# Last feed-forward layer: gate and up of 18 blocks as a 2x2 block product with seven multiplications

## The chip, the cores and the metric

One core of a Trainium2 chip runs the whole program in one launch. The metric is device time in microseconds (us). The kernel before took 1428.83 us, the median of three runs (1427.67 to 1429.59). The engines are TensorE (PE, with its weight loads PEld), VectorE (DVE), ScalarE (ACT), GpSimd (POOL) and SyncE (SP, which issues the weight loads); each works through its own queue in order.

## The reference

Two residual layers over a sequence of 512 rows of width 1024: an even layer (Mamba-2 scan and differential attention), an odd layer (S5 scan and latent attention), and behind each a SwiGLU feed-forward block; a final RMSNorm ends it. What the change touches is the second feed-forward block:

```
def rms_norm(x, g):
    y = xf * lax.rsqrt(jnp.mean(xf * xf, axis=-1, keepdims=True) + NORM_EPS)
    return (y * g.astype(F32)).astype(x.dtype)
def swiglu(x, wg, wu, wd):
    return (jax.nn.silu(x @ wg) * (x @ wu)) @ wd
h = h + swiglu(rms_norm(h, norm_ffn[i]), ffn_gate[i], ffn_up[i], ffn_down[i])
```

The hidden width is 2816, which is 22 blocks of 128. All arrays are float32.

## The kernel before

**Tiles.** The activations lie transposed: `h[i]`, i = 0..7, holds 128 features by 512 rows. A float32 product is made of three TensorE products: each operand is split into a high part in the format float32r and the remainder (`wsplit` for weights, `split_x` for activations: ScalarE casts, VectorE subtracts), and `mm3` adds hi·hi, hi·lo and lo·hi in one PSUM bank (L178, L179, L180). The operands of the feed-forward block are h times the gain, not yet normalised; the factor 1/rms of each row (`rbc`) is multiplied in afterwards.

**Units.** The work is a list of units. A unit is one output tile of 128 features by 512 rows: eight k-steps of three matmuls, 24 matmuls of 512 columns. Gate and up of one hidden block are two units. `ev_g` multiplies the gate by `rbc` on VectorE, applies SiLU on ScalarE, and multiplies by `rbc` on GpSimd (`padd`, L305); `ev_u` multiplies up and gate on VectorE, and `split_x` makes `hid{j}` of it. The 22 blocks go in three parts of 8, 7 and 7 (`PARTS`); behind each part the down projection adds its share to `h`. In the last part the first down unit is 512 columns wide and the others come as 256-column halves, with transposes, the final norm and the stores between them (`last_down`, `last_norm`, `finish`).

**Weights.** `wload` brings the weights of one hidden block, gate and up, as one DMA of 1 MB into one of two `raw` tiles (a row per partition: 1024 columns of gate, then 1024 of up). `wsplit` writes to `whi` and `wlo`, two buffers each; down weights with a `keep` number go to tiles `kh1..7` and `kl1..7` of the pool `fin`, which hold them for both halves.

**Order.** `drive` goes through the list and calls `prep` (load and split) for the next unit before `compute` of this one. This is only the order in which the instructions are written. The order within each engine's queue is made when the program is built: a planner plays the program through with durations of its own and gives each engine the earliest-written instruction that is ready by then, so later-written work can go ahead of earlier work that waits. What comes out of it is fixed; on the chip an engine does not change it.

Of the kernel before, what the change touches and what calls it, by code (L numbers as in the profile page):

```python
# [9 lines left out]
F32 = mybir.dt.float32  # L10
F32R = mybir.dt.float32r
# [7 lines left out]
P = 128  # L19
# [87 lines left out]


PARTS = (8, 7, 7)
CHUNKS = _chunks()  # L110
CH, WLEN = {}, {}
for _k, (_f, _p) in CHUNKS.items():
# [9 lines left out]
class Trunk:  # L122
    def __init__(self, ctx, tc, a, out):
        self.ctx, self.tc, self.nc, self.a, self.out = ctx, tc, tc.nc, a, out
        self.n = 0
# [28 lines left out]
    def wload(self, key):  # L154
        flat, off, n = CH[key]
        raw = self.t(self.wraw, [P, 2048], "raw")
        self.nc.sync.dma_start(out=raw[:, :sum(n)],
                               in_=self.a[flat][off:off + P * sum(n)].rearrange("(p n) -> p n", p=P))
        return raw

    def wsplit(self, raw, o, nk, cw, keep=None):
# [29 lines left out]

    def prep(self, u):
        if "w" in u:
            return
        if u["keep"] in self.kept:
            u["w"] = self.kept[u["keep"]]
            return
        if u["key"] not in self.raws:
            self.raws[u["key"]] = self.wload(u["key"])
        o = sum(CH[u["key"]][2][:u["sub"]])  # L200
        self.left[u["key"]] -= 1
        u["w"] = self.wsplit(self.raws[u["key"]], o, u["nk"], u["m"], u["keep"])
        if u["keep"] is not None:
            self.kept[u["keep"]] = u["w"]
# [48 lines left out]
    def drive(self, items):  # L253
        us = [x for x in items if isinstance(x, dict)]
        nxt = {id(u): v for u, v in zip(us, us[1:])}
        seen = set()
        for u in us:
            if u["keep"] is None or u["keep"] not in seen:
                self.left[u["key"]] = self.left.get(u["key"], 0) + 1
            seen.add(u["keep"])  # L260
        self.order = list(self.left)
        self.prep(us[0])
        for x in items:
            if isinstance(x, dict):
                if id(x) in nxt:
                    self.prep(nxt[id(x)])
                self.fetch()
                self.compute(x)
            else:
                x()  # L270
        self.flush()
# [122 lines left out]
    def setup(self):  # L394
# [9 lines left out]
        nc.gpsimd.memset(self.t(pad, [P, PAD], "pad")[:, 0:1], 0.0)  # L404
        self.pp = {n: self.pool(ctx, "ps_" + n, b, PSUM) for n, b in (("mm", 2), ("sc", 2), ("tp", 2), ("po", 2))}
        self.n_unit = 0
        self.raws, self.kept, self.left = {}, {}, {}
        self.queue, self.held = [], None
        self.cst_sb = self.t(cp, [P, NCST], "cst")
        self.par_sb = self.t(cp, [P, NPAR], "par")  # L410
# [561 lines left out]
        return items  # L972


    def ffn(self, l, E, gain, back=None):
        nc, a = self.nc, self.a
        V, A, G = nc.vector, nc.scalar, nc.gpsimd
# [2 lines left out]
        F = {}  # L980
        st2 = E["st2"] = {"acc": None}
        mt = ("mm", "sc")

        def start():
            F["p"] = self.pool(ctx, f"ff{l}")
            self.norm_done(E)

        def ev_g(j, ps):
# [5 lines left out]
        def ev_u(j, ps):  # L994
            gt = F["gt", j]
            V.tensor_tensor(out=gt, in0=ps, in1=gt, op=ALU.mult)  # L996
            F["hid"].append(self.split_x(F["p"], f"hid{j}", gt, None))
        items, j0 = [], 0
        for pi, nj in enumerate(PARTS):
# [3 lines left out]
            for j in range(nj):  # L1003
                items += [self.unit(f"g{l}_{j0 + j}", n, xs8, (lambda ps, j=j, e=e: e(j, ps)), mt)
                          for n, e in enumerate((ev_g, ev_u))]
                if back is not None:
                    items.append(back)
# [6 lines left out]
            if last and gain == "nfin":  # L1014
                def du(i, hfs):
# [30 lines left out]
    def last_norm(self, i, hf):  # L1046
        nc, st = self.nc, self.fin
        h = self.h[i][:, 256 * hf:256 * hf + 256]
        hg = self.t(self.finp, [P, 256], "hg", bufs=3)
        nc.scalar.activation(out=hg, in_=h, func=AF.Identity, scale=self.par("nfin", i))  # L1050
        sq = self.t(self.finp, [P, 256], f"fsq{hf if i == 0 else 2 + i % 2}")
        if i == KD - 1:
            nc.vector.tensor_tensor(out=sq, in0=h, in1=h, op=ALU.mult)
        else:
# [499 lines left out]
        return items  # L1554


@with_exitstack
def tile_trunk(ctx, tc, a, out):
    k = Trunk(ctx, tc, a, out)
# [18 lines left out]
    def open_fin():  # L1578
        c2.close()
        k.finp = k.pool(c4, "fin")  # L1580
        k.otm = k.t(k.finp, [P, 4, D], "otm")
# [97 lines left out]
```

## Time and profile before

| | us |
|---|---|
| median of the runs | 1428.83 |
| the profiled execution, its own time | 1427.25 |
| its span, from the first to the last instruction | 1425.4 |
| TensorE busy in the span | 1378.2 |
| VectorE busy | 932.9 |
| ScalarE busy | 665.0 |
| GpSimd busy | 225.4 |

The profile is of one execution. Times in the rows are microseconds unless marked ns. A matmul's duration includes its way through the array, so successive matmuls overlap; how fast they follow one another is read from their starts. The waits name what ended an engine's idle time.

### The profile page before, as it was taken

To read this page: it belongs to the slowest core of one execution; us is meant where nothing else is said; L and a number is where in the kernel's file an instruction comes from. 1 tells how busy PE (TensorE), PEld (TensorE's weight loads), DVE (VectorE), ACT (ScalarE), POOL (GpSimd) and SP (SyncE) were. 2 spreads that over 40 slices of the span, in tenths; PEclk is the share of its full clock that TensorE was granted. 3 is DMA by queue.
4 is the path that set the end of the run, shared out by engine and by line. 5 is a ranking of instruction groups with operands and counts; after the bars stand their busy time and mean duration, and the time that the engine had idled before them with its cause. 6 is when DMAs were issued, how large, how long until landed. Compare 5 with 4: busy or idle time off the path is not lost.

```text
span 1425.4 us, 18242 instructions
## 1 busy us (share of the span) xinstructions
PE 1378.2 (97%) x6947; PEld 1136.5 (80%) x6947; DVE 932.9 (65%) x1936; ACT 665.0 (47%) x1177; POOL 225.4 (16%) x184
## 2 busy tenths in 40 slices
PE   8999999999999989999999998989999999999997
PEld 5877878888888868887888786766788888888887
DVE  6987888878766994336766678887663433343454
ACT  7658787967643442233324432278452312222242
POOL 0234500000003101011011214510031101101111
PEclk9999999999999999999999999999999999999999
DMA  5221121121222222232232233220132232232221
GB/s 187 77 78 60 60 89 60 45 74 60 89 89 106 89 83 96 92 115 74 90 109 73 99 113 93 74 78 30 60 118 89 89 112 95 86 107 89 98 95 59
DMA packets 26102, 124.07 MB, mean 87 GB/s; under 512 B 3056, under 2 KB 7792, under 8 KB 14880
## 3 DMA queue, kind: packets, MB, share of 16 engines
q1 hardware_dynamic: 24656, 121.09, 24.7%
q10 hardware_dynamic: 1360, 1.83, 0.4%
q8 instruction: 54, 0.88, 0.3%
q14 instruction: 32, 0.26, 0.1%
HBM read 118.71 MB, written 4.19 MB: 86 GB/s over the span
## 4 chain that ended last, share of the span: by engine, by line
PE 71%; DVE 19%; ACT 5%; issue 2%; POOL 1%; DMA 1%; SPq 0%; ACTq 0%; DVEq 0%; POOLq 0%
PE mm L178 14%; PE mm L179 13%; PE mm L180 13%; PE sc L180 7%; PE sc L179 7%; PE sc L178 7%; DVE wlo L170 3%; DVE qsw L634 2%; ACT whi L169 1%; PE sc L1444 1%; PE po L879 1%; POOL xs L305 1%; ACT qsw L790 1%; PE po L1470 1%; PE mm L774 1%
## 5 line engine op out<-in xcount | busy, mean ns | idle before, releaser
L169 ACT CAST whi<-raw 128x1024 fp32r<-128x1024 f32 (+5 forms) x231 | 224.1, 970 | 530.3 <-PE mm L179 286.2
L170 DVE TENSOR_TENSOR wlo<-raw,whi 128x1024 fp32r<-128x1024 f32 (+5 forms) x231 | 263.3, 1140 | 32.4 <-ACT whi L169 22.6
L305 POOL TENSOR_TENSOR gt<-gt,rbc 128x512 f32<-128x512 f32 x44 | 76.2, 1732 | 573.1 <-ACT gt L991 573.1
L305 POOL TENSOR_TENSOR sacc<-sacc,sq 128x512 f32<-128x512 f32 x29 | 45.4, 1564 | 394.1 <-ACT sq L292 381.6
L996 DVE TENSOR_TENSOR gt<-mm,gt 128x512 f32<-128x512 f32 x44 | 30.4, 690 | 106.6 <-PE mm L180 103.3
L990 DVE TENSOR_TENSOR gt<-sc,rbc 128x512 f32<-128x512 f32 x44 | 30.4, 690 | 83.1 <-PE sc L180 83.0
L1011 DVE TENSOR_TENSOR h<-h,mm 128x512 f32<-128x512 f32 x20 | 13.7, 686 | 54.3 <-PE mm L180 54.3
L178 PE MATMUL mm<-x0h,whi 128*128 128x512 f32 (+2 forms) x91 | 39.1, 429 | 9.5 <-ACT whi L169 6.3
L1011 DVE TENSOR_TENSOR h<-h,sc 128x512 f32<-128x512 f32 x20 | 13.7, 687 | 47.2 <-PE sc L180 47.2
L180 PE MATMUL mm<-x0h,wlo 128*128 128x512 f32 (+2 forms) x91 | 36.8, 404 | 3.6 <-DVE wlo L170 3.6
L991 ACT ACTIVATE gt<-gt 128x512 f32<-128x512 f32 x44 | 27.6, 627 | 23.5 <-DVE gt L990 23.5
L790 ACT ACTIVATE qsw<-mm 32x512 f32<-32x512 f32 x64 | 37.7, 589 | 1.0 <-DVE qraw L786 0.2
L178 PE MATMUL mm<-x7h,whi 128*128 128x512 f32 (+2 forms) x95 | 37.1, 390 | 0.0
L180 PE MATMUL mm<-x7h,wlo 128*128 128x512 f32 (+2 forms) x95 | 37.0, 390 | 0.0
L179 PE MATMUL mm<-x7l,whi 128*128 128x512 f32 (+2 forms) x95 | 37.0, 389 | 0.0
L179 PE MATMUL mm<-x0l,whi 128*128 128x512 f32 (+2 forms) x91 | 36.6, 403 | 0.0
L178 PE MATMUL mm<-x1h,whi 128*128 128x512 f32 (+2 forms) x91 | 36.1, 396 | 0.0
L180 PE MATMUL mm<-x1h,wlo 128*128 128x512 f32 (+2 forms) x91 | 36.0, 395 | 0.0
L179 PE MATMUL mm<-x1l,whi 128*128 128x512 f32 (+2 forms) x91 | 36.0, 395 | 0.0
L178 PE MATMUL mm<-x2h,whi 128*128 128x512 f32 (+2 forms) x91 | 35.9, 395 | 0.0
L179 PE MATMUL mm<-x3l,whi 128*128 128x512 f32 (+2 forms) x91 | 35.6, 392 | 0.3 <-DVE x3l L365 0.3
L179 PE MATMUL mm<-x2l,whi 128*128 128x512 f32 (+2 forms) x91 | 35.9, 394 | 0.0
(938 smaller groups left out, 4294.7 us busy)
## 6 DMA issues: line engine op xcount, KB each, us to landing
raw<-in_f_dram SPq DMA_DIRECT2D x52, 1024.0 KB, 4.9
raw<-in_w_dram SPq DMA_DIRECT2D x35, 1024.0 KB, 4.9
raw<-in_f_dram SPq DMA_DIRECT2D x16, 896.0 KB, 4.4
raw<-in_w_dram SPq DMA_DIRECT2D x8, 512.0 KB, 3.5
h<-in_xt_dram SPq DMA_DIRECT2D x8, 256.0 KB, 5.2
regroup<-us SPq DMA_DIRECT2D x8, 256.0 KB, 2.0
raw<-in_w_dram SPq DMA_DIRECT2D x2, 640.0 KB
u<-regroup SPq DMA_DIRECT2D x16, 64.0 KB, 2.5
```

Of the source, the lines that this page charges most:

```text
L169: nc.scalar.copy(out=hi[:, :n], in_=raw[:, o:o + n])
L170: nc.vector.tensor_tensor(out=lo[:, :n], in0=raw[:, o:o + n], in1=hi[:, :n].bitcast(F32), op=ALU.subtract)
L178: nc.tensor.matmul(ps, lhsT=hi[:, k, :m], rhs=xh, start=start and j == 0, stop=False)
L179: nc.tensor.matmul(ps, lhsT=hi[:, k, :m], rhs=xl, start=False, stop=False)
L180: nc.tensor.matmul(ps, lhsT=lo[:, k, :m], rhs=xh, start=False, stop=stop and j == n - 1)
L305: self.nc.gpsimd.tensor_tensor(out=out, in0=x, in1=y, op=op)
L634: V.scalar_tensor_tensor(out=acc, in0=xr[:, 1 + k:1 + k + T], scalar=self.par("cw", 12 * k + j), in1=acc, op0=ALU.mult, op1=ALU.add)
L790: A.activation(out=sw[c * 32:(c + 1) * 32, :], in_=ps[d * 32:(d + 1) * 32, :], func=AF.Identity, scale=scale)
L990: V.tensor_tensor(out=gt, in0=ps, in1=E["rbc"], op=ALU.mult)
L991: A.activation(out=gt, in_=gt, func=AF.Silu)
L996: V.tensor_tensor(out=gt, in0=ps, in1=gt, op=ALU.mult)
L1011: V.tensor_tensor(out=self.h[i], in0=self.h[i], in1=ps, op=ALU.add)
```

## The change

The first four blocks (`NPLAIN`) stay as they were. For the other 18, with the weights of a block as four quarters G1, G2 (gate, features 0 to 511 and 512 to 1023) and U1, U2 (up), and the normalised activations as four quarters "11", "12" (features 0 to 511; rows 0 to 255 and 256 to 511) and "21", "22", both outputs come from seven products of 512 features by 256 rows: a Winograd form of Strassen's scheme. Each product is 4 k-steps of three matmuls of 256 columns, 12 matmuls; seven make 84.

- The seven activation operands are made once (`operands`): 16 multiplications by gain and `rbc`, four sums, and seven splits of 128x1024, woven between the plain units; they lie in `kh1..7` and `kl1..7`. `rbc` is in the operands, so `ev_g`'s two multiplications by it go in these 18 blocks.
- The weight operands are G1, G2, U2, and the sums S1 = U1+U2, U1+G1, S1+G1, and G2+S1+G1. S1 and U1+G1 are made by loads: SP loads U1 twice, and GpSimd's queue issues two loads that add U2 and G1 to what lies there (`add_sums`), for block J+1 where block J is prepared; the plain loads (`ask_sums`, `ask_first`, `ask_last`) are for block J+2. The two other sums are made on VectorE. In all seven quarter loads of 256 KB per block take the place of one load of 1 MB (for the first two fast blocks G1 and G2 come by `wload`, 1024 columns wide).
- Weight operands are split in four calls per block, in turn to `whi`/`wlo` (two buffers) and a third pair `ohi`/`olo`.
- A block is four units: a (products 1 and 2, 24 matmuls), c (product 5, 12), b (7 and 6, 24) and d (4 and 3, 24). Those of two blocks alternate: a(j), c(j-1), b(j), d(j-1). Partial results stay in PSUM: X (tag `mm`, two banks) from a to d, Y (`sc`) from b to d; three are copied out by ScalarE in between (`x1`, `y`, `u2`), three additions are made on VectorE.
- The pool of the final stage's tiles is opened after the fast blocks (`open_out`).

```diff
+    def open_out(self, ctx, fast):
+        fast.ctx.close()
+        self.otp = self.pool(ctx, "ot")
+        self.otm = self.t(self.otp, [P, 4, D], "otm")
...
+            if fast is not None and pi == 0:
+                us = us[:2] + self.weave(us[2:-1], [fast.ask] + fast.operands(self.par, gain_in)) + [fast.add] + us[-1:]
+            items += us
+            if n0 < nj:
+                items += fast.sets(range(n0, nj), j0)
...
+class FastPair:
...
+        def norm(i):
+            if i == 0:
+                alloc()
+            h, q = i // 4, i % 4
+            for n in range(2):
+                c = slice(256 * n, 256 * n + 256)
+                V.scalar_tensor_tensor(out=t[f"{h + 1}{n + 1}"][:, 256 * q:256 * q + 256], in0=k.h[i][:, c],
+                                       scalar=par(gain, i), in1=E["rbc"][:, c], op0=ALU.mult, op1=ALU.mult)
...
+        fs = [lambda i=i: norm(i) for i in range(8)]
+        fs += [lambda: diff("t1", "11", "12", self.p, "olo"), lambda: split(5, "t1", 1),
+               lambda: nsum("t2", "t1", "22", k.finp, "kl7"), lambda: split(6, "t2", 2),
+               lambda: diff("t3", "22", "12", None, "12"), lambda: split(7, "t3", 3), lambda: split(3, "22", 4),
+               lambda: split(1, "11", 5), lambda: nsum("t4", "t2", "21", None, "t1"), lambda: split(4, "t4", 6),
+               lambda: split(2, "21", 7)]
...
+    def split(self, *srcs):
...
+        pool, tags = (k.whl, ("whi", "wlo")) if self.n_op % 3 != 1 else (self.p, ("ohi", "olo"))
+        self.n_op += 1
...
+    def ask_sums(self, j):
...
+        s["s1"] = k.t(self.p, [P, 512], "s1", bufs=3)
+        s["s32"] = k.t(self.p, [P, 1024], "s32", bufs=3)
+        for out in (s["s1"], s["s32"][:, 0:512]):
+            k.nc.sync.dma_start(out=out, in_=self.src(j, 1024))
...
+    def add_sums(self, j):
+        k, s = self.k, self.st[j]
+        for out, c in ((s["s1"], 1536), (s["s32"][:, 0:512], 0)):
+            k.nc.gpsimd.dma_start(out=out, in_=self.src(j, c), accum_op=ALU.add)
...
+        for j in range(4):
+            for i, (y, x) in enumerate(((hi, xh), (hi, xl), (lo, xh))):
+                nc.tensor.matmul(ps[:, 0:256], lhsT=y[:, b + j, :], rhs=x[:, j, :], start=start and i + j == 0,
+                                 stop=i + j == 5, skip_group_check=not start)
...
+        def make_a(j, prev):
...
+                if prev is not None:
+                    make_s1(self.st[j0 + prev])
+                if J + 1 < NH:
+                    self.add_sums(J + 1)
+                V.tensor_tensor(out=s["s32"][:, 512:1024], in0=s["s1"], in1=r1, op=ALU.add)
+                V.tensor_tensor(out=s["s4"][:, 512:1024], in0=r2, in1=s["s32"][:, 512:1024],
+                                op=ALU.add)
+                if J + 2 < NH:
+                    self.ask_sums(J + 2)
+                    self.ask_first(J + 2)
+                if prev is None:
+                    s["w3"] = self.split(s["s32"])
+                return (w,)
...
+        def a(j):
+            def f_(w):
+                s = self.st[j0 + j]
+                s["X"], z = k.ps("mm"), k.ps("tp")
+                self.prod(s["X"], w, 0, 1, True)
+                x1 = self.copy("x1", ("x1l", "x2h"), s["X"])
+                self.prod(z, w, 4, 2, True)
+                s["gt"] = k.t(F["p"], [P, T], "gt", bufs=2)
+                V.tensor_tensor(out=s["gt"][:, 0:256], in0=z[:, 0:256], in1=x1, op=ALU.add)
+                A.activation(out=s["gt"][:, 0:256], in_=s["gt"][:, 0:256], func=AF.Silu)
+            return f_
...
+        def b(j):
...
+                s["Y"] = k.ps("sc")
+                self.prod(s["Y"], w, 0, 7, True)
+                s["y"] = self.copy("y", ("x2l", "x3h"), s["Y"])
+                self.prod(s["X"], w, 4, 6)
+                s["u2"] = self.copy("u2", ("x3l", "x4h"), s["X"])
...
+        def c(j):
...
+                self.prod(s["X"], w, 0, 5)
+                s["ut"] = self.x2("ut", ("x4l", "x5h"), 512)
+                V.tensor_tensor(out=s["ut"][:, 256:512], in0=s["X"][:, 0:256], in1=s["y"], op=ALU.add)
...
+        def d(j):
...
+                self.prod(s["Y"], w, 0, 4)
+                V.tensor_tensor(out=ut[:, 0:256], in0=s["Y"][:, 0:256], in1=s["u2"], op=ALU.add)
+                self.prod(s["X"], w, 4, 3)
+                A.activation(out=gt[:, 256:512], in_=s["X"][:, 0:256], func=AF.Silu)
+                V.scalar_tensor_tensor(out=gt, in0=gt, scalar=-1.0, in1=ut, op0=ALU.mult, op1=ALU.mult)
+                F["hid"].append(k.split_x(F["p"], f"hid{j}", gt, None))
...
+            p = js[i - 1] if i else None
+            out.append(unit(j, make_a(j, p), a(j), early))
+            if p is not None:
+                out.append(unit(p, (lambda _, p=p: make_s1(self.st[j0 + p])), c(p)))
+            out.append(unit(j, make_b(j), b(j)))
+            if p is not None:
+                out.append(unit(p, make_d(p), d(p)))
```

## Rows read from the trace of the kernel before

**Rows 1.** The page: span, busy time of the engines, share of it.

```profile
span 1425.4 us, 18242 instructions
PE 1378.2 (97%) x6947; PEld 1136.5 (80%) x6947; DVE 932.9 (65%) x1936; ACT 665.0 (47%) x1177; POOL 225.4 (16%) x184
```

**Rows 2.** Busy time by stretch: blocks 0 to 3, then part two's gate and up.

```profile
core 0: us, PE busy (x) PEld busy (x) DVE busy (x) ACT busy (x) POOL busy (x), PEclk, DMA share, GB/s
1048.35:1091.90 43.55, 43.55 (x201) 36.34 (x200) 20.68 (x32) 15.31 (x19) 9.76 (x6) 1.00 0.28 99
1186.19:1262.00 75.81, 75.81 (x336) 62.80 (x335) 30.91 (x36) 22.41 (x29) 12.43 (x7) 1.00 0.27 94
```

**Rows 3.** Waits, 1048 to 1426 us: engine, for whom, total, times, longest.

```profile
ACT whi L169 <- PE mm L179: 111.2, 29, 5.3
...
ACT kh L169 <- DMA raw<-in_f_dram: 0.9, 1, 0.9
```

**Rows 4.** TensorE's timeline, one block of 512 columns: start, duration, instruction.

```profile
1180.76 0.39 PE L178 MATMUL sc<-x0h,whi 128*128 128x512 f32 x1
...
1185.97 0.39 PE L180 MATMUL sc<-x7h,wlo 128*128 128x512 f32 x1
...
1191.63 0.39 PE L178 MATMUL sc<-x0h,whi 128*128 128x512 f32 x1
```

**Rows 5.** TensorE's timeline, the down halves: 256 columns, transposes in between.

```profile
1375.91 0.28 PE L178 MATMUL mm<-hid0h,kh 128*128 128x256 f32 x1
...
1378.31 0.28 PE L180 MATMUL mm<-hid6h,kl 128*128 128x256 f32 x1
...
1379.04 0.28 PE L179 MATMUL mm<-hid0l,kh 128*128 128x256 f32 x1
1379.35 0.44 PE L1064 MATMUL tp<-cst,hg 128*128 128x128 f32 x2
1379.54 0.37 PE L180 MATMUL mm<-hid0h,kl 128*128 128x256 f32 x1
```

**Rows 6.** Groups by line and shape, VectorE, last feed-forward layer: busy, mean ns.

```profile
L170 DVE TENSOR_TENSOR wlo<-raw,whi 128x1024 fp32r<-128x1024 f32 x51 | 62.7, 1229 | 12.1 <-ACT whi L169 8.2 <-PE tp L350 3.2
L996 DVE TENSOR_TENSOR gt<-mm,gt 128x512 f32<-128x512 f32 x22 | 15.2, 692 | 68.2 <-PE mm L180 66.0 <-POOL gt L305 2.1
L1041 DVE TENSOR_TENSOR h<-h,mm 128x256 f32<-128x256 f32 x14 | 5.9, 421 | 21.6 <-PE mm L180 21.6
```

**Rows 7.** Groups by line and shape, ScalarE, last feed-forward layer.

```profile
L169 ACT CAST whi<-raw 128x1024 fp32r<-128x1024 f32 x51 | 53.7, 1054 | 194.0 <-PE mm L179 95.8 <-PE sc L179 90.4 <-PE mm L180 4.1
L991 ACT ACTIVATE gt<-gt 128x512 f32<-128x512 f32 x22 | 13.8, 626 | 0.0
L1055 ACT ACTIVATE fsq<-h 128x256 f32<-128x256 f32 x14 | 5.6, 402 | 0.0
```

**Rows 8.** Timeline, VectorE beside GpSimd, and the start of the layer.

```profile
1050.60 1.37 POOL L305 TENSOR_TENSOR sacc<-sacc,sq 128x512 f32<-128x512 f32 x1 [0.86 <-ACT sq L292]
1050.74 1.77 DVE L368 SCALAR_TENSOR_TENSOR x7l<-h,par,x7h 128x512 fp32r<-128x512 f32 x1
...
1061.24 0.59 ACT L354 COPY rbc<-tp 128x512 f32<-128x512 f32 x1
```

**Rows 9.** Timeline, VectorE's sequence where a unit ends.

```profile
1186.39 0.69 DVE L990 TENSOR_TENSOR gt<-sc,rbc 128x512 f32<-128x512 f32 x1 [3.36 <-PE sc L180]
...
1192.75 1.22 DVE L170 TENSOR_TENSOR wlo<-raw,whi 128x1024 fp32r<-128x1024 f32 x1 [0.15 <-ACT whi L169]
1193.89 0.68 DVE L365 TENSOR_TENSOR hid0l<-gt,hid0h 128x512 fp32r<-128x512 f32 x1
```

**Rows 10.** The tile raw: duration ns min/median/max, first and last start.

```profile
L169 ACT CAST kh<-raw x7: 929/938/945, 1356.4 to 1376.2; 128x896 fp32r<-128x896 f32 x7
```

**Rows 11.** DMA issues by kind: count, KB each, median us to landing.

```profile
raw<-in_f_dram SPq DMA_DIRECT2D x52, 1024.0 KB, 4.9
regroup<-us SPq DMA_DIRECT2D x8, 256.0 KB, 2.0
```

More of the change, by code (lines that the diff above doesn't have):

```diff
@@ L109 @@
 PARTS = (8, 7, 7)
+NPLAIN = 4
 CHUNKS = _chunks()
@@ L156, in wload @@
         raw = self.t(self.wraw, [P, 2048], "raw")
-        self.nc.sync.dma_start(out=raw[:, :sum(n)],
-                               in_=self.a[flat][off:off + P * sum(n)].rearrange("(p n) -> p n", p=P))
+        w = 1024 if key in self.fast else sum(n)
+        self.nc.sync.dma_start(out=raw[:, :w],
+                               in_=self.a[flat][off:off + P * sum(n)].rearrange("(p n) -> p n", p=P)[:, :w])
         return raw
@@ L193, in prep @@
         if "w" in u:
+            return
+        if "make" in u:
+            if u["key"] is not None:
+                if u["key"] not in self.raws:
+                    self.raws[u["key"]] = self.wload(u["key"])
+                self.left[u["key"]] -= 1
+            u["w"] = u["make"](self.raws.get(u["key"]))
             return
@@ L257, in drive @@
         for u in us:
-            if u["keep"] is None or u["keep"] not in seen:
+            if u["key"] is not None and (u["keep"] is None or u["keep"] not in seen):
                 self.left[u["key"]] = self.left.get(u["key"], 0) + 1
@@ L406, in setup @@
         self.n_unit = 0
-        self.raws, self.kept, self.left = {}, {}, {}
+        self.raws, self.kept, self.left, self.fast = {}, {}, {}, set()
         self.queue, self.held = [], None
@@ L982, in ffn @@
         mt = ("mm", "sc")
+        gain_in = f"nf{l}"
         def start():
             F["p"] = self.pool(ctx, f"ff{l}")
+            if fast is not None:
+                fast.open()
             self.norm_done(E)
@@ L998, in ffn @@
         items, j0 = [], 0
+        fast = FastPair(self, l, E, F) if gain == "nfin" else None
         for pi, nj in enumerate(PARTS):
@@ L1002, in ffn @@
             items.append(lambda: F.__setitem__("hid", []))
-            for j in range(nj):
-                items += [self.unit(f"g{l}_{j0 + j}", n, xs8, (lambda ps, j=j, e=e: e(j, ps)), mt)
-                          for n, e in enumerate((ev_g, ev_u))]
-                if back is not None:
-                    items.append(back)
+            n0 = nj if fast is None else NPLAIN if pi == 0 else 0
+            us = []
+            for j in range(n0):
+                us += [self.unit(f"g{l}_{j0 + j}", n, xs8, (lambda ps, j=j, e=e: e(j, ps)), mt)
+                       for n, e in enumerate((ev_g, ev_u))]
+                if back is not None:
+                    us.append(back)
+            if fast is not None and pi == 0:
[3 more added lines that the diff above has]
+                items += fast.sets(range(n0, nj), j0)
             last = pi == len(PARTS) - 1
@@ L1014, in ffn @@
             if last and gain == "nfin":
+                items.append(lambda: self.open_out(ctx, fast))
                 def du(i, hfs):
@@ L1048, in last_norm @@
         h = self.h[i][:, 256 * hf:256 * hf + 256]
-        hg = self.t(self.finp, [P, 256], "hg", bufs=3)
+        hg = self.t(self.otp, [P, 256], "hg", bufs=3)
         nc.scalar.activation(out=hg, in_=h, func=AF.Identity, scale=self.par("nfin", i))
-        sq = self.t(self.finp, [P, 256], f"fsq{hf if i == 0 else 2 + i % 2}")
+        sq = self.t(self.otp, [P, 256], f"fsq{hf if i == 0 else 2 + i % 2}")
         if i == KD - 1:
```

120 lines of the change are left out of this document (119 added, 1 removed).

## The prediction

> **What bounds the kernel now.** I read the page's busy shares first: TensorE is busy for 97% of the span, VectorE for 65%, ScalarE for 47% [rows 1]. Then the table by stretch, to see whether that holds where the change is made: in the gate and up units of the last layer TensorE has no idle time at all (43.55 of 43.55 us and 75.81 of 75.81), its granted clock is 1.00 (the level of 2.4 GHz), VectorE is busy for 41 to 47%, and the DMA engines for 27 to 28% [rows 2]. The waits agree: ScalarE and VectorE wait for matmuls (111.2 us in 29 waits is one pair alone), and a wait for a load ends last once, for 0.9 us [rows 3]. So in this stretch time is the number of matmuls times the distance between their starts, and every microsecond taken from TensorE's queue is gained until another engine, a bank or a load is late.
>
> **The change part by part.**
>
> *TensorE's columns.* A block is now 48 matmuls of 512 columns; from its first to the next block's first go 1191.63 - 1180.76 = 10.87 us, or 0.2265 us each [rows 4]. After, it is 84 of 256 columns. The down halves show that distance: 20 steps in 1378.31 - 1375.91 = 2.40 us, so 0.120 us, with other weights in every matmul, as in the fast blocks [rows 5]. 84 x 0.120 = 10.08 us. Halving the columns leaves 53% of the time, not 50%: of the 12.5% fewer columns only 7.3% of time remain as gain, 0.79 us per block, 14.2 us in 18 blocks. That is all that the change can give, unless matmuls follow each other faster than in these rows.
>
> A page of the Trainium skill gives the distance otherwise ("TensorE: Matmul & The Clock Gate", section "Back-to-back issue gap"): columns / 2.4 plus 2.5 ns for a lone stream at full clock, so 216 and 109 ns. By it a block would go from 10.36 to 9.17 us, an estimate of 21 us gained in 18 blocks. The trace does not agree: 226.5 and 120 ns stand in the rows, some 11 ns more for either size, and these count against the smaller matmul twice as often.
>
> *The activation operands, in the plain blocks.* They cannot start before `rbc`, which is there at 1061.24 + 0.59 = 1061.83 [rows 8]; four plain blocks from 1048.35 [rows 2] end after 4 x 10.87 us at 1091.84, so VectorE has 30.0 us. Its added work is 16 multiplications of 256 columns, four sums of 1024 and seven low parts of 1024. Full-length operations follow each other at 1193.89 - 1192.75 = 1.14 us [rows 9], less than the duration of 1.23 [rows 6]; the 256-column ones I take at 0.40 (0.42 for an addition of that size, rows 6). 16 x 0.40 + 11 x 1.14 = 18.9 us. VectorE's own work in that time is about five weight splits and ten 512-column operations at 1.14 and 0.62 (0.69 less the same overlap): 11.9 us. The sum, 30.8 us, is already over 30.0, and it is a chain (each low part waits for ScalarE's cast of 1.05 us, rows 7; the operands "21" and the last sum reuse tiles of earlier ones). Also a VectorE operation of two SBUF inputs beside a GpSimd one took 1.77 us [rows 8], where one of 512 columns takes 0.69 [rows 6]: the GpSimd multiplication by `rbc` stays in these four blocks, one each. Behind it come the first fast block's weight split and sums (some 3 us of VectorE), part of which is needed at once. I expect the first fast block to start 3 to 5 us late and take 4; the ends are 0 (the planner packs it all) and 8 (each GpSimd multiplication costs one more microsecond). Up to 4 us of it has no cover: TensorE has nothing else to do there.
>
> *VectorE in a fast block.* Low parts: two of 512, one of 512 (S1), two of 1024: 3 x 0.69 + 2 x 1.23. Sums in SBUF: 2 x 0.69. Three additions from PSUM of 256: 3 x 0.42. The last product and the hidden block's low part: 2 x 0.69. Together 8.6 us by duration [rows 6], about 7.7 at the distances of rows 9, against 10.08 of TensorE. Before it was 30.91 / 7 = 4.4 [rows 2]. *ScalarE*: casts of 2 x 0.62, 0.62 and 2 x 1.05, three copies and two SiLU of 256 columns at 0.40, the hidden cast 0.62: 6.6 us [rows 7]. Neither is the bound, but VectorE goes from 41% to some 80%. *GpSimd* loses its 18 multiplications, which nobody waited for.
>
> *The buffers.* In TensorE time a block is a (0 to 2.9), c (to 4.3), b (to 7.2), d (to 10.1). Three pairs of split weights go round, so each split has from the end of the unit that used its buffer to the start of its own: 4.3 us for the two of 1024 columns, 5.8 for a and S1. One split needs 1.05 + 1.23 = 2.3 us on two engines in turn. That leaves 2 us for whatever is ahead in the queues, so this is hidden as long as no engine is blocked for longer.
>
> *The bank of X.* X holds a bank from a(j) to the SiLU behind d(j), there are two, and d(j) stands right before a(j+2), whose first product wants the same bank. A unit's evacuation begins 1186.39 - 1185.97 = 0.42 us after its last matmul starts [rows 4, 9], some 0.31 for 256 columns (0.28 duration, rows 5); with a SiLU of 0.40 and the way back of about 0.05 the bank is free 0.76 us after that start, 0.64 later than the next matmul could go. Bare, that is 11.5 us in 18 blocks. But a's second product goes to another bank and its weights are ready, and the planner does let later-written matmuls go first: in the down halves two matmuls of the next unit run ahead of the transposes that were written before them and waited [rows 5]. Five or six matmuls of product 2 fill the gap. What is left is where the plan is off: there, the transposes start 1379.35 - 1379.04 - 0.12 = 0.19 us late. I take 0.1 per block, 1.8 us; the ends are 0 and 11.5.
>
> *The loads.* 1.75 MB per block instead of 1 MB: the DMA share of 0.28 becomes about 0.5, which is bandwidth enough. A load of 256 KB landed in 2.0 us, one of 1 MB in 4.9 [rows 11], so SP's five plain loads per block have several times their need. No accumulating load is in the trace. Bounds by the nearest rows: the two of a block together land no sooner than one plain 256 KB load, 2.0 us, and I put the upper end at twice a 1 MB load, 9.8 us, since each also reads and rewrites its destination. I take 5 us, the 1 MB row. They are written one block (10 us) ahead of the VectorE sum that waits for them, and on GpSimd's queue nothing is behind them. So they cost nothing, if the planner does not pull that sum forward (the last rival). The DMA page ("DMA: Bandwidth & Descriptors", section "Anatomy of one DMA") has 2.0 us plus bytes over 436 GB/s for a load from GpSimd's queue, an estimate of 2.6 us each; no run here shows it.
>
> *Borders and the tail.* Five changes between fast blocks and down units, with split buffers that come free one unit before their use: 0.2 each, 1 us (0 to 3). The seven kept down weights were split up to 20 us ahead, between 1356.4 and 1376.2 [rows 10]; their tiles now hold operands until the last fast block ends. The first down unit then gives 21 x 0.2265 = 4.8 us for the first ones, at 1.1 each, and each following half takes over 2.5: hidden, though without the old lead.
>
> *Sum.* -14.2 + 4 + 1.8 + 1 = -7.4 us. The profiled execution took 1427.25 (span 1425.4 and 1.85 around it); it would become 1419.85. The median of the runs lies 1.58 above it: 1428.83 - 7.4 = 1421.4.
>
> **The rivals.**
> (1) Nothing is lost: the planner packs the operands and the bank, 1428.83 - 14.2 = 1414.6, to 1417. For it: no idle time at all in the units before [rows 2]; against it: VectorE's 30.8 in 30.0 us. Chance 0.18.
> (2) The distance of the 256-column matmuls is shorter than in the rows. If it halved with the columns, to 0.113 us, 84 x 0.007 x 18 = 10.6 us more would go: 1411. The 20 steps of rows 5 are against it: 0.02. The rule of the clock-gate page above comes to nearly that halving.
> (3) The bank of X is not covered: 0.64 instead of 0.1 per block, +9.7 us, 1431, no change that can be measured. 0.12.
> (4) VectorE becomes the bound: GpSimd's issuing of two loads per block disturbs it as the GpSimd operation in rows 8 did, 1.0 us each: 8.6 + 2.0 = 10.6 us per block against 10.08, +9.4 us, 1431. 0.10.
> (5) Slower: the accumulating loads hold VectorE. The planner goes by durations of its own and pulls work forward as soon as it reckons its data there (the kept splits, 20 us early, rows 10), and it was wrong once: ScalarE then stood 0.9 us for a load [rows 3]. If the sum on S1 is placed in VectorE's queue before its load has landed, all behind it waits: the low parts of the weights, the PSUM additions, the hidden block, and by them TensorE. It decides from about 2 us of lateness, the slack of the split buffers; each microsecond beyond costs 18 us. At 3 us late: 1421.4 + 18 = 1439. For it: no row shows these loads; against: a whole block of lead. 0.16.
> The forecast has the remaining 0.42; its own range is 1417 to 1426.
>
> **How the numbers follow.** Changes within 0.2% (2.9 us, 1426.0 to 1431.7) cannot be told from none. Faster: 0.18 + 0.02 + 0.40 of the forecast, 0.07 of (3) and (4) = 0.67. Same: 0.02 + 0.07 + 0.02 of (5) = 0.11. Slower: 0.08 of (3) and (4), 0.14 of (5) = 0.22. The range leaves out (2) and the far half of (5): 1414 to 1440.
>
> **What would show it.** TensorE's starts in a fast block at 0.120 us and 10.1 us from a(j) to a(j+1); one idle stretch of TensorE of 3 to 5 us near 1092 that ends on VectorE's low part of an operand or a weight; a few matmuls of product 2 between d and the first of product 1, or else a gap there that ends on the SiLU (rival 3). VectorE at about 80% and none of its waits ended by a DMA; if the waits list VectorE behind the accumulating loads for over 2 us per block, rival 5 is true. If VectorE has no idle time in the fast blocks and its operations are stretched, rival 4. The prediction is wrong if a block takes over 10.6 us, or if the start costs over 8.

## The result, and the profile after

The changed kernel takes 1445.77 us (median of 4 runs, 1443.47 to 1447.23), slower than before: ratio 1.0118 [1.0106, 1.0131]. The forecast was 1421.4. The profiled execution took 1446.81 us, with a span of 1445.0.

The page of the changed kernel: span, busy time, the DMA queues (packets, MB, share of the engines' time), and the accumulating loads (count, KB each, median us from issue to landing).

```profile
span 1445.0 us, 20118 instructions
PE 1377.6 (95%) x7595; PEld 1161.1 (80%) x7595; DVE 1012.2 (70%) x2087; ACT 721.3 (50%) x1308; POOL 232.0 (16%) x202
q1 hardware_dynamic: 34736, 125.81, 25.1%
q0 software_dynamic: 5184, 9.44, 3.9%
s<-in_f_dram POOLq DMA_DIRECT2D x36, 256.0 KB, 4.7
```

Beside [rows 1], TensorE is busy for as long as before and idle for 20 us more. It lost time in two places, which one cut separates: the first matmul of the last feed-forward layer (`sc<-x0h`), here before and after.

```profile
1048.35 0.39 PE L178 MATMUL sc<-x0h,whi 128*128 128x512 f32 x1
```

```profile
1059.15 0.39 PE L180 MATMUL sc<-x0h,whi 128*128 128x512 f32 x1
```

So 10.8 us are gone before the layer begins (1.7 of them already at 335 us, where TensorE's order of work is still that of before). From there to the end of the span it is 377.05 us before and 385.85 after. The layer itself, which was to become 7.4 us shorter, became 8.8 longer.

**The loss before the layer.** Timelines of GpSimd, ScalarE and TensorE in the changed kernel, at the end of the odd layer: start, duration, instruction, and in brackets the idle time before it with what ended it ("issue": nothing that the profile shows).

```profile
1032.96 1.91 POOL L1670 DMA_DIRECT2D s<-in_f_dram  x2 [87.01 <-DMA s<-in_f_dram]
1036.01 0.86 POOL L1670 DMA_DIRECT2D s<-in_f_dram  x1 [1.14 <-DMA s<-in_f_dram]
1042.59 0.88 POOL L1670 DMA_DIRECT2D s<-in_f_dram  x1 [5.73 <-issue]
...
1045.06 1.59 POOL L314 TENSOR_TENSOR sacc<-sacc,sq 128x512 f32<-128x512 f32 x1
...
1046.68 0.63 ACT L301 ACTIVATE sq<-h 128x512 f32<-128x512 f32 x1 [8.61 <-POOL sacc L314]
1047.22 0.60 ACT L171 CAST whi<-raw 128x512 fp32r<-128x512 f32 x1
...
1047.87 0.79 PE L180 MATMUL mm<-cx,whi 128*128 128x512 f32 x1 [5.85 <-ACT whi L171]
```

Read it upwards. TensorE waits 5.85 us for a weight's high part; ScalarE has it in its queue behind a square (`sq`), which waits 8.61 us for a buffer that GpSimd's statistics addition (`sacc`) frees. That addition stands behind accumulating loads of the first product blocks, and GpSimd stands for 5.73 us before it can issue one of these. Before, the same additions came every 2.72 us (1036.99, 1039.71, 1042.43). After the stall TensorE also ran at a low clock. Busy time by stretch:

```profile
core 0: us, PE busy (x) PEld busy (x) DVE busy (x) ACT busy (x) POOL busy (x), PEclk, DMA share, GB/s
1039.00:1047.80 8.80, 3.02 (x14) 2.17 (x12) 0.69 (x1) 1.12 (x3) 4.19 (x5) 0.94 0.97 236
1047.80:1054.00 6.20, 5.81 (x14) 4.17 (x15) 4.62 (x6) 3.38 (x7) 4.16 (x3) 0.54 0.30 51
```

The granted clock is 0.54 in the 6 us behind the stall, close to the lower level of 1.2 GHz, where it was 1.00 [rows 2].

**The loss in the layer.** Waits of VectorE and TensorE in the changed kernel (total, times, longest):

```profile
DVE s L1737 <- DMA s<-in_f_dram: 32.1, 9, 5.8
PE sc L1699 <- DVE wlo L1652: 11.5, 5, 4.8
```

and one of them in the timelines of VectorE, SP, GpSimd and TensorE:

```profile
1128.39 0.68 DVE L1652 TENSOR_TENSOR olo<-s,ohi 128x512 fp32r<-128x512 f32 x1
...
1129.10 1.79 SPq L1665 DMA_DIRECT2D s<-in_f_dram  x2
...
1132.94 0.86 POOL L1670 DMA_DIRECT2D s<-in_f_dram  x1 [6.82 <-DMA s<-in_f_dram]
...
1136.92 0.69 DVE L1737 TENSOR_TENSOR s<-s,x0h 128x512 f32<-128x512 f32 x1 [5.78 <-DMA s<-in_f_dram]
1137.53 1.22 DVE L1652 TENSOR_TENSOR wlo<-s,whi 128x1024 fp32r<-128x1024 f32 x1
...
1138.81 0.57 PE L1699 MATMUL sc<-kh,wlo 128*128 128x256 f32 x1 [4.75 <-DVE wlo L1652]
```

VectorE's own low part of S1 (1128.39) frees a buffer; only then does SP issue the two plain loads of a later block; GpSimd waits 6.82 us for one of them before it issues the accumulating load (1132.94); VectorE stands until this has landed (1136.92). The sum that it stands for belongs to block 8, whose matmuls come after the down units and begin at 1201.39:

```profile
1201.39 0.28 PE L1699 MATMUL mm<-kh,whi 128*128 128x256 f32 x1
```

Behind it in the queue (1137.53) is the low part of block 5's last weight operand, which TensorE wants at once. So the load has no lead at all: VectorE frees the buffer, and then waits for everything that follows from that. And the wait costs more than its own length. Behind it, too, TensorE ran near the lower level, with a granted clock of 0.51 (columns as in the table above):

```profile
1138.81:1142.20 3.39, 3.39 (x16) 3.39 (x17) 3.39 (x7) 1.20 (x3) 0.00 (x0) 0.51 0.32 107
```

### The profile page after: what moved, and what is told of

It reads as the page before. It is cut to its first block, busy times and chain, and to the rows that moved or that the text cites. A ratio compares the mean times of both kernels' runs of the same rounds, so it can differ in the third digit from the quotient of the medians.

```text
span 1445.0 us, 20118 instructions
## 1 busy us (share of the span) xinstructions
PE 1377.6 (95%) x7595; PEld 1161.1 (80%) x7595; DVE 1012.2 (70%) x2087; ACT 721.3 (50%) x1308; POOL 232.0 (16%) x202
## 3 DMA queue, kind: packets, MB, share of 16 engines
q1 hardware_dynamic: 34736, 125.81, 25.1%
q0 software_dynamic: 5184, 9.44, 3.9%
## 4 chain that ended last, share of the span: by engine, by line
PE 63%; DVE 21%; ACT 5%; DMA 4%; issue 3%; POOL 3%; SPq 0%; DVEq 0%; ACTq 0%; POOLq 0%
PE mm L180 11%; PE mm L181 10%; PE mm L182 10%; PE mm L1699 5%; PE sc L181 4%; PE sc L182 4%; PE sc L180 4%; DVE wlo L172 4%; DMA s<-in_f_dram 3%; PE sc L1699 3%; DVE qsw L643 1%; PE sc L1471 1%; PE tp L1699 1%; ACT whi L171 1%; PE po L888 1%
## 5 line engine op out<-in xcount | busy, mean ns | idle before, releaser
L171 ACT CAST whi<-raw 128x1024 fp32r<-128x1024 f32 (+5 forms) x195 | 186.1, 954 | 361.1 <-PE mm L181 203.8
L172 DVE TENSOR_TENSOR wlo<-raw,whi 128x1024 fp32r<-128x1024 f32 (+5 forms) x195 | 220.3, 1130 | 34.7 <-ACT whi L171 25.4
L1699 PE MATMUL mm<-kh,whi 128*128 128x256 f32 x196 | 56.8, 290 | 0.4 <-DVE gt L1013 0.3
L1699 PE MATMUL mm<-kh,wlo 128*128 128x256 f32 x196 | 55.8, 285 | 1.3 <-DVE wlo L1652 1.3
L1699 PE MATMUL mm<-kl,whi 128*128 128x256 f32 x196 | 55.7, 284 | 0.0
L1651 ACT CAST whi<-s 128x1024 fp32r<-128x1024 f32 (+1 forms) x36 | 32.1, 892 | 37.6 <-PE mm L1699 33.4
L1652 DVE TENSOR_TENSOR wlo<-s,whi 128x1024 fp32r<-128x1024 f32 (+1 forms) x36 | 37.0, 1028 | 12.8 <-ACT whi L1651 12.6
L1699 PEld LDWEIGHTS mm<-kh,whi 128*128 128x128 f32 x196 | 37.8, 193 | 2.8 <-ACT gt L1800 1.3
L1699 PEld LDWEIGHTS mm<-kh,wlo 128*128 128x128 f32 x196 | 37.8, 193 | 1.8 <-DVE wlo L1652 1.8
L1699 PE MATMUL sc<-kh,wlo 128*128 128x256 f32 x92 | 27.2, 295 | 11.5 <-DVE wlo L1652 11.5
L1699 PEld LDWEIGHTS mm<-kl,whi 128*128 128x128 f32 x196 | 37.8, 193 | 0.1
```

What stands on the lines that cost most here:

```text
L171: nc.scalar.copy(out=hi[:, :n], in_=raw[:, o:o + n])
L172: nc.vector.tensor_tensor(out=lo[:, :n], in0=raw[:, o:o + n], in1=hi[:, :n].bitcast(F32), op=ALU.subtract)
L1651: k.nc.scalar.copy(out=hi[:, c], in_=x)
L1652: k.nc.vector.tensor_tensor(out=lo[:, c], in0=x, in1=hi[:, c].bitcast(F32), op=ALU.subtract)
L1699: nc.tensor.matmul(ps[:, 0:256], lhsT=y[:, b + j, :], rhs=x[:, j, :], start=start and i + j == 0, stop=i + j == 5, skip_group_check=not start)
```

## The experiments

Each ran beside the kernel before on the same chip (three chips for these runs), so runs of different groups are compared by ratio. "Layer start" is the first matmul `sc<-x0h` and "layer" the time from there to the end of the span, from the profiled executions.

```
run               median us  ratio to before [95%]     layer start  layer
before                                                     1048.35  377.05
after               1445.77  1.0118 [1.0106, 1.0131]       1059.15  385.85
e1_pool_after       1439.88  1.0083 [1.0066, 1.0100]       1049.39  388.4
e2_sums_late        1429.53  1.0010 [1.0001, 1.0020]       1057.01  370.0
e3_both             1421.26  0.9953 [0.9939, 0.9968]       1048.70  370.0
e6_no_sums          1425.60  0.9984 [0.9975, 0.9993]       1049.71  373.6
e7_ring             1440.77  1.0081 [1.0066, 1.0096]       1051.00  386.1
e8_no_sums_late     1421.42  0.9945 [0.9929, 0.9962]       1049.73  370.0
e9_plain5           1420.63  0.9942 [0.9927, 0.9957]       1049.68  369.3
e10_plain6          1419.58  0.9932 [0.9917, 0.9947]       1048.32  368.3
e11_best            1417.88  0.9929 [0.9917, 0.9942]       1049.53  366.6
e12_lead            1439.87  1.0084 [1.0068, 1.0099]       1049.88  388.5
```

**e1_pool_after: the accumulating loads behind the statistics on GpSimd's queue.**

```diff
-            self.padd(st["acc"], st["acc"], sq)
+            self.last_sacc = self.padd(st["acc"], st["acc"], sq)
...
-            k.nc.gpsimd.dma_start(out=out, in_=self.src(j, c), accum_op=ALU.add)
+            with k.tc.issue_after(k.last_sacc.ins):
+                k.nc.gpsimd.dma_start(out=out, in_=self.src(j, c), accum_op=ALU.add)
```

> The accumulating loads are queued on GpSimd behind the last addition to the sum of squares of the layer's input norm; nothing else is changed. Theory A (two queues are held by work that was pulled forward: GpSimd's before the layer, 9 us, and VectorE's in it, 13 us): the stall before the layer and the half-clock stretch behind it go, 1445.8 - 9 = 1437 us (1434 to 1440), and the VectorE waits for the loads stay at about 32 us. Theory B (the loads themselves are too slow for this kernel, wherever they are queued): the stall only moves into the plain blocks, 1443 to 1447.

Measured 1439.88, ratio 1.0083. The layer starts at 1049.39: the first loss is gone with one edit of order. The layer itself is no better (388.4), and the waits of VectorE and TensorE on this path are still there:

```profile
DVE s L1738 <- DMA s<-in_f_dram: 29.3, 6, 6.1
PE sc L1700 <- DVE wlo L1652: 12.0, 5, 4.9
```

By the ratios (1.0118 and 1.0083) the whole run gains 5 us, and not the 9.8 of the layer's start; in the profiled execution the layer became 2.5 us longer. The longer stalls make up 0.9 of this. Most of the rest is the clock: in the changed kernel TensorE runs near the lower level once in this layer, and here it does so twice. This is the second time (columns as in the table by stretch above):

```profile
1335.10:1338.40 3.30, 3.30 (x18) 3.30 (x17) 3.16 (x6) 1.24 (x4) 0.00 (x0) 0.50 0.46 161
```

**e2_sums_late: the two SBUF sums behind the last PSUM addition of the unit before, on VectorE's queue.**

```diff
-                V.tensor_tensor(out=s["s32"][:, 512:1024], in0=s["s1"], in1=r1, op=ALU.add)
...
+                with ExitStack() as e:
+                    if self.last is not None:
+                        e.enter_context(k.tc.issue_after(self.last.ins))
+                    V.tensor_tensor(out=s["s32"][:, 512:1024], in0=s["s1"], in1=r1, op=ALU.add)
...
-                V.tensor_tensor(out=s["ut"][:, 256:512], in0=s["X"][:, 0:256], in1=s["y"], op=ALU.add)
+                self.last = V.tensor_tensor(out=s["ut"][:, 256:512], in0=s["X"][:, 0:256], in1=s["y"], op=ALU.add)
...
```

`self.last` is set in c, as shown, and likewise in d.

> VectorE's sum on top of an accumulated sum is queued behind the PSUM addition of unit c (or d) that was written last before it, so it can't go ahead by more than about a block; GpSimd's queue is as in the changed kernel. Theory A: VectorE's waits for the loads fall from 32 to under 8 us, TensorE's stalls on low parts by 13 us, 1445.8 - 13 = 1433 us (1430 to 1437), the stall before the layer stays. Theory B: the sums are late where they are needed too, units b wait as long as before, 1441 to 1447.

Measured 1429.53, ratio 1.0010, a little better than either theory gave. The layer takes 370.0 us, 15.9 less than in the changed kernel (whose five listed stalls of TensorE sum to 11.5; shorter stalls and the low clock are in the rest), and no wait of VectorE for a load of `s` is left among the waits. The loss before the layer stands as it was:

```profile
1046.25 0.79 PE L180 MATMUL mm<-cx,whi 128*128 128x512 f32 x1 [5.79 <-ACT whi L171]
```

**e3_both: both orders.** The edits of the two runs above, together.

> Both orders of the two runs before. Theory A: the gains add, 1445.8 - 22 = 1424 us (1420 to 1428), which is under the kernel before (1428.7). Theory B: 1440 to 1447. If the product of smaller matmuls itself costs more than its rows say (theory C): 1429 to 1436, with no waits for loads left.

Measured 1421.26, ratio 0.9953 [0.9939, 0.9968]; the forecast's 7.4 us would be 0.9948. It is faster than either kernel. The two losses are separate and the order of two queues is all of the slowdown. This run shows the rest of the prediction undisturbed. From its profile: TensorE where one block meets the next, twice; the waits of TensorE's weight loads there, for the SiLU (`gt`) that frees a bank of X (total, times, longest); and three of the stalls at the start of the product form.

```profile
1210.49 0.28 PE L1701 MATMUL tp<-kl,ohi 128*128 128x256 f32 x1
1210.76 0.39 PE L1701 MATMUL mm<-kh,ohi 128*128 128x256 f32 x1
1210.98 0.28 PE L1701 MATMUL mm<-kl,ohi 128*128 128x256 f32 x1
...
1220.81 0.28 PE L1701 MATMUL tp<-kl,whi 128*128 128x256 f32 x1
1221.07 0.39 PE L1701 MATMUL mm<-kh,whi 128*128 128x256 f32 x1
```

```profile
PEld mm L1701 <- ACT gt L1805: 2.4, 12, 0.2
```

```profile
1090.53 0.50 PE L182 MATMUL mm<-x0h,wlo 128*128 128x512 f32 x1 [1.30 <-DVE wlo L172]
1096.81 0.39 PE L1701 MATMUL mm<-kh,wlo 128*128 128x256 f32 x1 [0.73 <-DVE wlo L1653]
...
1101.62 0.38 PE L1701 MATMUL mm<-kh,wlo 128*128 128x256 f32 x1 [0.63 <-DVE wlo L1653]
```

Matmuls of 256 columns start 0.12 us apart, a block takes 1220.81 - 1210.49 = 10.32 us, and around the first product of a new block the starts are 0.27 and 0.22 us apart, together 0.25 us lost. Such a gap stands 12 times in the layer, not 18: twice in the four blocks of the first part and five times in each of the other parts (from 1115.88, 1200.44 and 1310.32 on), always from a part's third block on: there are two banks, and the first two blocks of a part find one free. The stalls at the start, measured from start to start, are 1.45, 0.90, 0.48, 0.79 and 0.33: 3.95 us.

**e6_no_sums: no accumulating loads, the planner's order.** It leaves out the loads, so the sums that they make are missing.

```diff
-            k.nc.gpsimd.dma_start(out=out, in_=self.src(j, c), accum_op=ALU.add)
+            pass
```

> Leaves out the accumulating loads (the sums that they make are not made; all else runs as in the changed kernel, the loads of SP too). It bounds what these loads cost in all. Theory A: 1445.8 - 9 - 13 = 1424 us, as with both orders (1419 to 1427); theory B the same. Theory C: 1430 or more, since it has nothing to do with the loads.

Measured 1425.60, ratio 0.9984: slower than with the loads and the right order. With no accumulating load in the program VectorE still stands for plain ones, 12 times for the 9 of the changed kernel, each time for less:

```profile
DVE s L1737 <- DMA s<-in_f_dram: 37.5, 12, 3.8
```

The layer takes 373.6 us, so of the 15.9 the planner's order costs 3.6 with plain loads alone. The other 12.3 come with the second transfer in series.

**e8_no_sums_late: no accumulating loads, the sums in their place.** The edits of e6 and e2 together.

> This leaves out the 36 accumulating loads (so the sums are wrong halves) and keeps the mended order of VectorE's additions. Without them and with the planner's order it took 1425.6, and with them and both orders mended 1421.3. Theory A: it is the place of the two additions on VectorE's queue, pulled ahead of a split that TensorE waits for, that makes any late load cost, a plain one too; once they are in place, even the accumulating loads cost nothing: 1421.3 within 1 us. Theory B: accumulating loads also cost something that order does not mend (transfer engines, port): then 1418 to 1420.

Measured 1421.42, ratio 0.9945, layer 370.0 us, to a tenth that of e3_both. Theory A: in its place on the queues, an accumulating load costs nothing, though the DMA engines are far busier with it. From 1200 to 1250 us of either (columns as in the table by stretch above), e8 first:

```profile
1200.00:1250.00 50.00, 49.97 (x409) 49.02 (x408) 35.66 (x56) 29.23 (x54) 0.00 (x0) 1.00 0.39 127
```

```profile
1200.00:1250.00 50.00, 49.97 (x409) 49.02 (x408) 36.73 (x57) 28.44 (x54) 8.72 (x10) 1.00 0.74 185
```

The accumulating loads take the DMA share from 0.39 to 0.74, and TensorE is busy for 49.97 us of 50 in both.

**e7_ring: the scratch memory of GpSimd's issues doubled, nothing else.**

```diff
-    nc = _bacc.Bacc("TRN2", target_bir_lowering=False, num_devices=1, dynamic_dma_scratch_size=1024)
+    nc = _bacc.Bacc("TRN2", target_bir_lowering=False, num_devices=1, dynamic_dma_scratch_size=2048)
```

> The changed kernel with the scratch memory from which GpSimd issues its transfers doubled (1024 to 2048), nothing else. In the changed kernel's trace GpSimd issues three accumulating loads, then sits for 5.73 us with no releaser named ("issue"), and the statistics addition that the next weight split waits for is behind them on its queue. In the run with both orders mended the same shows harmlessly, three issues together and then 4.13 us of "issue". Theory A: the issues use up the scratch memory, and the fourth has to wait until an earlier transfer has landed. Then with twice the memory the wait before the fourth goes, the addition comes up to 6 us earlier, and the time falls by 3 to 6 us: 1439 to 1443. Theory B: GpSimd waits for its loads' plain partners, or for the crowded transfer engines (0.95 busy in that stretch), whatever the memory: then the wait stands where it is and the time stays within 1 us of 1445.

Measured 1440.77, ratio 1.0081, inside theory A's range. GpSimd's timeline:

```profile
1032.47 1.92 POOL L1670 DMA_DIRECT2D s<-in_f_dram  x2 [86.87 <-DMA s<-in_f_dram]
1035.69 0.86 POOL L1670 DMA_DIRECT2D s<-in_f_dram  x1 [1.30 <-DMA s<-in_f_dram]
...
1038.23 0.86 POOL L1670 DMA_DIRECT2D s<-in_f_dram  x1 [0.39 <-DMA s<-in_f_dram]
1038.79 1.60 POOL L314 TENSOR_TENSOR sacc<-sacc,sq 128x512 f32<-128x512 f32 x1
```

The "issue" wait of 5.73 us is gone, the addition comes 6.3 us earlier (1038.79 for 1045.06) and the layer starts at 1051.00. The DMA engines were no less crowded (0.89 busy from 1028 to 1050, 0.83 in the changed kernel), so it was the room for issued transfers that ran out, and not the engines. The loss in the layer is untouched (386.1).

**e12_lead: GpSimd's order mended, each accumulating load issued with its plain one.**

```diff
         self.add_sums(NPLAIN)
+        self.add_sums(NPLAIN + 1)
...
-                if J + 1 < NH:
-                    self.add_sums(J + 1)
...
                 if J + 2 < NH:
                     self.ask_sums(J + 2)
+                    self.add_sums(J + 2)
```

> GpSimd's order mended and VectorE's left as the planner has it (as in the first run, 1439.9), with one difference: each accumulating load is issued together with its plain one, two blocks ahead, and not one block ahead. Theory A: what costs is that the planner pulls the two additions ahead of the splits on VectorE's queue, to where one of their loads has not landed; with the accumulating loads earlier they wait only for the plain loads, as in the run without accumulating loads: 1425 to 1429. Theory B: the accumulating loads are late because they are slow or crowded, whenever they are issued: then the waits stay and the time is 1437 to 1441.

Measured 1439.87, ratio 1.0084, layer 388.5: nothing changed against e1, and the time lies in theory B's range. But the edit did not test what it was to test. GpSimd's issues in this run, and then the same two in e1_pool_after:

```profile
1107.87 0.88 POOL L1671 DMA_DIRECT2D s<-in_f_dram  x1 [6.96 <-DMA s<-in_f_dram]
1122.56 0.86 POOL L1671 DMA_DIRECT2D s<-in_f_dram  x1 [6.10 <-DMA s<-in_f_dram]
```

```profile
1107.04 0.87 POOL L1671 DMA_DIRECT2D s<-in_f_dram  x1 [6.62 <-DMA s<-in_f_dram]
1123.44 0.86 POOL L1671 DMA_DIRECT2D s<-in_f_dram  x1 [6.23 <-DMA s<-in_f_dram]
```

The issues stand where they stood, within 0.9 us, because GpSimd was already waiting for the plain load each time. What the run does show: the place of the accumulating load in the text sets nothing; the plain load before it does, and that waits for VectorE's own split. Another buffer of each of the two tiles might give a real lead; that was not tried.

**e9_plain5 and e10_plain6: both orders, and five or six plain blocks in place of four.**

```diff
-NPLAIN = 4
+NPLAIN = 5        # e10_plain6: 6
```

> Both orders mended, and five plain blocks ahead of the product form in place of four. The four stalls of TensorE at the start of the product form (1.45, 0.90, 0.48, 0.79 and 0.33 us in the run with both orders mended, 3.95 in all) stand behind VectorE, which works without a break from 1062 to 1086 on the operands. One more plain block costs 10.87 - 10.31 = 0.56 us and gives VectorE that much longer for the operands. Theory A: VectorE's pile-up is the cause; with a block more the stalls go, or mostly: 1421.3 - 3.9 + 0.6 = 1418.0, between 1417.5 and 1419.5. Theory B: the stalls come from the first product block's own splits, wherever it begins: 1421.8.

> As the one before, with six plain blocks. Theory A: no stall is left at five already, so six cost another 0.56 us: 1418.6. If five leave half of the stalls, six remove the rest: 1418.5 too, and the trace tells the two apart. Theory B: 1422.4.

Measured 1420.63 (ratio 0.9942) and 1419.58 (0.9932); the layer takes 369.3 and 368.3 us, after 370.0 with four. Theory A holds in sign, but its sizes were wrong. With five the stall of 1.46 us in the fourth block stayed and another came, behind ScalarE; with six only the first is left. TensorE of e9, then of e10:

```profile
1091.53 0.50 PE L182 MATMUL mm<-x0h,wlo 128*128 128x512 f32 x1 [1.30 <-DVE wlo L172]
1113.01 0.39 PE L1701 MATMUL mm<-kh,ohi 128*128 128x256 f32 x1 [0.99 <-ACT x1l L1706]
```

```profile
1090.16 0.50 PE L182 MATMUL mm<-x0h,wlo 128*128 128x512 f32 x1 [1.30 <-DVE wlo L172]
```

**e11_best: six plain blocks, both orders, and the second multiplication by `rbc` of this layer on VectorE.**

```diff
-            self.padd(gt, gt, E["rbc"], ALU.mult)
+            (G if fast is None else V).tensor_tensor(out=gt, in0=gt, in1=E["rbc"], op=ALU.mult)
```

> Six plain blocks and both orders mended, and the second multiplication by the row scale (gt times rbc, 512 columns) of this layer's plain blocks on VectorE in place of GpSimd. With six plain blocks one stall is left at the start, 1.46 us at 1088.47, before the matmul that waits for a split of VectorE; that split stands behind 1.19 us in which VectorE waits for GpSimd's multiplication, which took 4.61 us there and 1.51 us where VectorE did other work. Theory A: GpSimd's long multiplication is the cause of the stall; on VectorE it takes 0.69 us, the wait and the stall go: 1419.6 - 1.4 = 1418.2, between 1417.4 and 1419.0. Theory B: VectorE is so full there that 0.69 us more on it costs what the wait gave, or puts another stall in its place: 1419.6 to 1420.6.

Measured 1417.88, ratio 0.9929 [0.9917, 0.9942]: inside theory A's range, and the lowest ratio of all. The multiplication in e10, on GpSimd, and what VectorE waited; then in e11, on VectorE:

```profile
1063.82 1.51 POOL L314 TENSOR_TENSOR gt<-gt,rbc 128x512 f32<-128x512 f32 x1 [1.04 <-ACT gt L1008]
1064.10 1.52 DVE L1616 SCALAR_TENSOR_TENSOR kl<-h,par,rbc 128x256 f32<-128x256 f32 x1
...
1081.91 4.60 POOL L314 TENSOR_TENSOR gt<-gt,rbc 128x512 f32<-128x512 f32 x1 [10.09 <-ACT gt L1008]
...
1086.55 0.69 DVE L1013 TENSOR_TENSOR gt<-mm,gt 128x512 f32<-128x512 f32 x1 [1.19 <-POOL gt L314]
```

```profile
1081.19 0.68 DVE L1009 TENSOR_TENSOR gt<-gt,rbc 128x512 f32<-128x512 f32 x1
1085.20 0.68 DVE L1013 TENSOR_TENSOR gt<-mm,gt 128x512 f32<-128x512 f32 x1
```

0.68 us on the fuller engine for 4.60 on the emptier one. The layer takes 366.6 us, and TensorE has no stall at the start any more. The ratios of e10 and e11 overlap, so the times alone don't show the gain over e10; the rows and the vanished stall do.

## Why the prediction was wrong

**The step that failed** is the one on the loads: "They are written one block (10 us) ahead of the VectorE sum that waits for them, and on GpSimd's queue nothing is behind them. So they cost nothing, if the planner does not pull that sum forward (the last rival)." Both halves failed, and each cost a loss of its own.

- *"On GpSimd's queue nothing is behind them."* True in the fast blocks, which is where I looked. But the loads of the first product blocks depend only on other loads, so the planner put them as early as the odd layer's end, ahead of the statistics additions there. I had costed the queue that the loads were written in, not the queue that they would be planned into. With the order mended the layer starts 9.8 us earlier (1059.15 to 1049.39). What made GpSimd stand was, for 5.73 us in one piece, the room for issued transfers (e7).
- *"One block ahead of the sum."* The lead is in the text only. On the queues the sum is up to 64 us ahead of its use (1136.92 against 1201.39), and the accumulating load is in a chain that begins at VectorE's own split and takes 8.5 us from it (1128.39 to 1136.92). I named this as rival 5 and gave it 0.16; the rows that spoke for it, kept splits up to 20 us early and one wait for a load [rows 3, 10], deserved more. The rival's size was about right by accident: 1439 forecast, 1439.9 with this loss alone (e1). It came as a few long stalls, five of TensorE of up to 4.9 us and the low clock behind them, not as the 1 us per block and microsecond that I worked with. My sign for it, over 2 us of VectorE's waits per block, was set too high as well: 32.1 us in 18 blocks is 1.8.

**What was right**, by e3_both, where both losses are away. The layer takes 370.0 us for the 369.65 that follow from the sum (377.05 - 7.4). That it is so close is partly luck: two terms, the bank and the borders, were wrong by about 1 us in opposite directions.

- *TensorE's columns*: 0.120 us from start to start, as read from the down halves [rows 5]. 14.2 us is the gain before the rest. The 21 us beside it came from a formula that the Trainium skill ("TensorE: Matmul & The Clock Gate", section "Back-to-back issue gap") gives for an isolated matmul, and not for a stream with a weight load for each matmul; the rows decide.
- *The start*: 3.95 us for 4 forecast, all of it behind VectorE and four of the five stalls behind its splits, as the working had it, though not in one stretch. The working had 30.8 us of VectorE in 30.0; two more plain blocks remove all but one stall of it, and that one was GpSimd's multiplication. Of this I had said that "each GpSimd multiplication costs one more microsecond"; it took up to 5.27 us. The Trainium skill ("SBUF — State Buffer", section "SBUF: two separate sides") says that a GpSimd operation that reads SBUF and a VectorE operation of two SBUF inputs share a pair of ports, which whichever starts first holds for its whole instruction. The trace agrees, both ways (e10): the multiplication of 1.51 us came between two VectorE operations, and the second of them took 1.52 us where its neighbours took 0.48; the one of 4.60 us ended 1.2 us after an unbroken row of VectorE operations of 1024 columns did (1085.35), so it was kept out through the whole row.
- *The bank of X*: 0.1 in each of 18 blocks forecast, 0.25 found in 12 of them; a block with the gap takes 10.32 us for 10.18. That is 12 x 0.25 = 3.0 us for 1.8.
- *Borders and the tail*: 1 us forecast. -14.2 + 3.95 + 3.0 = -7.25, and measured is 370.0 - 377.05 = -7.05, so 0.2 us remain for them.
- *VectorE in the fast blocks*: 36.73 of 50 us, 73% for about 80% forecast. Rivals 3 and 4 are out: no undisturbed block loses 0.64 us at the bank, and VectorE has idle time.
- *The landing of an accumulating load*: 5 us taken, 4.7 found in the changed kernel, between the bounds. The page of the Trainium skill that I quoted beside it ("DMA: Bandwidth & Descriptors", section "Anatomy of one DMA") gave an estimate of 2.6; the measurement decides. The DMA share was put at about 0.5 and came to 0.74, which cost nothing (e8).

The change as such is a gain of 0.5% (e3), 0.7% with six plain blocks and the multiplication moved (e11). As it stood it lost 1.2%, all of it to the places that two kinds of instruction had on their queues.

## What to carry to other kernels

A load hidden by "one block of lead" is hidden only if the consumer stands that late on its engine's queue. Where a planner orders the queues, ask for every instruction that waits for a transfer how early it could be placed, what is then behind it, and whether the buffer that the transfer fills is freed by the same engine. An instruction that depends on little can be placed early, even before the border of its stage, so look at what it passes there too, on the idlest engine above all. When a change loses, cut the trace at one matmul that both kernels have: the times before and after it told the two losses apart at once.

## What the runs showed of the hardware that I had not expected

- Accumulating loads from GpSimd use about twice the DMA time per byte: 3.9% of the span for 9.44 MB against 25.1% for 125.81 MB, 0.41 and 0.20% per MB. It is not the packets' size: of the packets of 2 KB in the changed kernel's trace, a median one took 178 ns in the accumulating loads and 84 on the plain queue.
- GpSimd issues three accumulating loads of 256 KB and then stands, 5.73 us in the changed kernel and 3.3 to 5.5 in the other runs, until there is room for the next; with twice the scratch memory it issued five without such a wait. The profile names no releaser for it.
- A GpSimd multiplication of 512 columns took from 1.51 to 5.27 us, by what VectorE did beside it.
- After 6 us without work TensorE's granted clock was 0.54 for the next 6 us, so that a stall of 5.85 us cost 9.1 (the 10.8 of the layer's start less the 1.7 from before).
